# A two-layer decoder trunk on one core: modulation slices summed by GpSimd and ScalarE, gates by VectorE, tokens scaled ahead of plain transposes

## The chip, the cores and the metric

The kernel runs on one core of a Trainium2 chip. The metric is device time in microseconds (us) of one execution. A difference below 0.3% (3.5 us) is treated as no difference. The engines are TensorE (PE in the rows, its weight loads PEld), VectorE (DVE), ScalarE (ACT), GpSimd (POOL) and SyncE (SP), whose queue issues nearly all loads.

## The reference, cut to what matters

One sequence of 256 tokens of width 1024 passes two layers. Each layer has a token mixer and a channel mixer, the second being a dense SwiGLU in layer 0 and eight experts of which each token takes two in layer 1. Ahead of each mixer the tokens are normed and modulated by a vector `c`:

```python
c_act = jax.nn.silu(c)
for layer in range(DEPTH):
    mod = c_act @ ada_w[layer] + ada_b[layer]
    sh_m, sc_m, gt_m, sh_f, sc_f, gt_f = [m[:, None, :] for m in jnp.split(mod, 6, axis=-1)]
    h = modulate(rms_norm(x, norm_mix_g[layer]), sh_m, sc_m)
    x = x + gt_m * hybrid_mixer(h, ...)
    h = modulate(rms_norm(x, norm_ffn_g[layer]), sh_f, sc_f)
    x = x + gt_f * (swiglu(h, ...) if layer % 2 == 0 else moe_swiglu(h, ...))
return rms_norm(x, final_g)
```

`c_act @ ada_w` is twelve products of a vector of 1024 with a matrix of 1024 x 1024: twelve slices, named by kind (`sh_m`, `sc_m`, `gt_m`, `sh_f`, `sc_f`, `gt_f`) and layer. A shift or scale is wanted as a column (features along partitions), a gate as a row spread over all partitions. All inputs are float32.

## The kernel before

**Tiling.** Every weight comes in units of 128 x 2048 numbers (1 MB), loaded by SP into a ring of six buffers `raw` in the order in which the program loads them. Apart from the modulation's, a unit is split in two halves of 1024 columns: ScalarE rounds a half into `whi` (L145), VectorE subtracts into `wlo` (L146), and TensorE takes three products (high by high, high by low, low by high) for each block of weights. Five `whi` and five `wlo` buffers stand between the splits and TensorE.

**Stages.** The front is startup, mixer 0 (ten units of `win`, gated linear attention and a recurrence, four units of `wout` in `residual`), the dense layer (eleven pairs of units `f1` and `f3`, then eleven units `f2` in `residual`), and mixer 1. The experts follow. Each `residual` ends with four blocks of twelve products; after each block VectorE multiplies by the gate (`y`, L440) and adds into the tokens `xs` (L441). For two token halves `norm` then squares and sums on ScalarE (`junk`, L338), adds on VectorE (`rs`, L344), takes the power on GpSimd (L345), and multiplies the identity by the result on VectorE (`dg`, L360). TensorE multiplies the tokens by `dg` (L364), which turns and scales them at once; ScalarE applies scale and shift (`h`, L377), VectorE splits into `wide_hi` and `wide_lo` (L380, L381), and the next mixer starts.

**Modulation.** A slice is four loads of 1 MB, its pieces. They are queued by `put`, and `fill(n)` takes n pieces at places given by the table FILLS. The table ON says who works a slice. Seven of the twelve are products on TensorE with `c` repeated in 32 columns (L261): each piece is four products, laid side by side in four column groups. Five are multiplied and added on VectorE, two instructions for a piece (L264, L266), and then summed over partitions by products with ones (L276, L286). A column slice ends in four small transposes (L226 into `pm`, from `row`), a gate in two products that spread it (L276 or L278).

**Order.** The program is written in one order; a scheduler moves instructions on each engine before the kernel is built, and each engine then runs its own list strictly in order. A GpSimd instruction or a ScalarE instruction whose input is late thus holds all that stand behind it.

## Time and profile before

| | us |
|---|---|
| median of 3 runs (1166.84 to 1169.84) | 1167.07 |
| the profiled execution | 1168.7 |
| its span, first to last instruction | 1166.9 |
| startup, until mixer 0's first `win` product | 44.07 |
| mixer 0, until its last product | 104.74 |
| wait and norm between mixer 0 and the dense layer | 9.66 |
| dense layer, until its last product | 197.08 |
| wait and norm between dense layer and mixer 1 | 14.20 |
| mixer 1 | 97.55 |
| experts and last norm | 699.60 |

The stages are cut at TensorE's instructions, and their times add up to the span. The profiled execution is 1.6 us above the median, and 1.8 us of its time lie outside its span. TensorE's share of busy time is 95% over the span; it is a busy share of records that overlap, so a saving is read from the stage in which it falls.

### The profile page before, as it was taken

What the parts mean: (1) busy time and instruction counts of PE and PEld (TensorE: products, weight loads), DVE (VectorE), ACT (ScalarE), POOL (GpSimd) and SP (SyncE); (2) the same over time, 40 slices, a digit from 0 to 9 for tenths busy, and PEclk for the clock granted to TensorE, in tenths of its full rate; (3) what the DMA queues carried; (4) which work ended last, traced back from release to release, by engine and by line L of the source; (5) the groups of instructions that cost most, each with busy time, mean ns of one, the idle gap of its engine ahead of it and who ended that gap; (6) DMA issues with size and microseconds to landing.
All of it is one profiled execution on the core that took longest, in us unless ns stands there. A gap on an engine that the chain in (4) does not pass through costs nothing.

```text
span 1166.9 us, 15801 instructions
## 1 busy us (share of the span) xinstructions
PE 1107.4 (95%) x6125; PEld 742.8 (64%) x6125; DVE 627.4 (54%) x818; ACT 518.3 (44%) x724; POOL 30.5 (3%) x69
## 2 busy tenths in 40 slices
PE   4899999999999999899999999999999999998993
PEld 2578779999777888686465445554455544655540
DVE  2668556757776765797135443353343633345442
ACT  2764444444437744786234333542342333434331
POOL 2000000000001000300000000000000000000000
PEclk9899999999999999899999999999999999998996
DMA  9977486858886447495999999999999999999994
GB/s 361 410 288 291 145 324 249 310 201 306 334 332 229 147 143 288 181 359 189 418 420 419 420 419 420 419 420 420 388 406 419 420 419 419 419 419 403 398 420 172
DMA packets 57182, 395.69 MB, mean 339 GB/s; under 512 B 8294, under 2 KB 8710, under 8 KB 9356
## 3 DMA queue, kind: packets, MB, share of 16 engines
q1 hardware_dynamic: 54272, 393.24, 84.2%
q10 hardware_dynamic: 2828, 1.37, 0.4%
q8 instruction: 50, 0.82, 0.3%
q14 instruction: 32, 0.26, 0.1%
HBM read 393.53 MB, written 1.05 MB: 338 GB/s over the span
## 4 chain that ended last, share of the span: by engine, by line
PE 88%; DMA 4%; ACT 3%; DVE 2%; POOL 1%; issue 1%; ACTq 0%; POOLq 0%; DVEq 0%; SPq 0%
PE pa L1050 17%; PE pa L158 8%; PE pa L157 8%; PE pa L159 8%; PE po L1099 7%; PE pa L406 6%; PE pa L407 6%; PE pa L408 6%; PE pb L158 4%; PE pb L159 4%; PE pb L157 4%; PE pm L226 2%; PE pb L261 2%; PE pm L973 2%; DMA bdx<-in_wx_dram 2%; ACT whi L145 2%
## 5 line engine op out<-in xcount | busy, mean ns | idle before, releaser
L146 DVE TENSOR_TENSOR wlo<-raw,whi 128x1024 fp32r<-128x1024 f32 x318 | 378.6, 1222 | 205.1 <-ACT whi L145 204.4
L145 ACT ACTIVATE whi<-raw 128x1024 fp32r<-128x1024 f32 x318 | 324.5, 1057 | 214.7 <-PE pa L407 90.2
L1050 PE MATMUL pa<-raw,x_n 128*64 128x512 f32 (+3 forms) x960 | 205.0, 562 | 0.0
L406 PE MATMUL pa<-wide_hi,whi 128*128 128x256 f32 x544 | 154.3, 284 | 0.2 <-DVE wide_hi L380 0.2
L407 PE MATMUL pa<-wide_lo,whi 128*128 128x256 f32 x544 | 153.5, 282 | 0.2 <-DVE wide_lo L381 0.2
L408 PE MATMUL pa<-wide_hi,wlo 128*128 128x256 f32 x544 | 153.5, 282 | 0.0
L1050 PEld LDWEIGHTS pa<-raw,x_n 128*64 128x64 f32 (+1 forms) x960 | 63.0, 131 | 106.7 <-issue 101.3
L158 PE MATMUL pa<-wlo,x_hi 128*128 128x512 f32 (+1 forms) x288 | 113.3, 394 | 3.7 <-DVE wlo L146 3.7
L157 PE MATMUL pa<-whi,x_hi 128*128 128x512 f32 (+1 forms) x288 | 110.7, 389 | 0.9 <-ACT whi L145 0.3
L159 PE MATMUL pa<-whi,x_lo 128*128 128x512 f32 (+1 forms) x288 | 109.9, 382 | 0.1
L406 PEld LDWEIGHTS pa<-wide_hi,whi 128*128 128x128 f32 x544 | 102.3, 188 | 6.4 <-issue 4.0
L407 PEld LDWEIGHTS pa<-wide_lo,whi 128*128 128x128 f32 x544 | 102.5, 189 | 1.6 <-issue 1.1
L408 PEld LDWEIGHTS pa<-wide_hi,wlo 128*128 128x128 f32 x544 | 102.5, 188 | 0.3 <-issue 0.3
L1099 PE MATMUL po<-raw,big 128*64 128x512 f32 (+1 forms) x440 | 93.4, 616 | 6.3 <-DMA raw<-in_m_dram 6.3
L1053 ACT ACTIVATE s<-pa 128x512 f32<-128x512 f32 (+1 forms) x30 | 16.9, 562 | 163.4 <-PE pa L1050 163.4
L158 PE MATMUL pb<-wlo,a_hi 128*128 128x512 f32 x176 | 71.6, 408 | 2.0 <-DVE wlo L146 2.0
L158 PEld LDWEIGHTS pa<-wlo,x_hi 128*128 128x128 f32 x288 | 55.3, 192 | 26.5 <-DVE wlo L146 6.7
L159 PE MATMUL pb<-whi,a_lo 128*128 128x512 f32 x176 | 69.8, 398 | 0.0
L157 PEld LDWEIGHTS pa<-whi,x_hi 128*128 128x128 f32 x288 | 55.3, 192 | 21.8 <-issue 7.7
L157 PE MATMUL pb<-whi,a_hi 128*128 128x512 f32 x176 | 60.8, 403 | 2.0 <-ACT whi L145 2.0
L1099 PEld LDWEIGHTS po<-raw,big 128*64 128x64 f32 (+1 forms) x440 | 25.4, 132 | 57.8 <-issue 49.8
L159 PEld LDWEIGHTS pa<-whi,x_lo 128*128 128x128 f32 x288 | 55.5, 193 | 10.0 <-DVE x_lo L986 0.8
(323 smaller groups left out, 1242.4 us busy)
## 6 DMA issues: line engine op xcount, KB each, us to landing
raw<-in_m_dram SPq DMA_DIRECT2D x263, 1024.0 KB, 10.6
raw<-in_ada_w_dram SPq DMA_DIRECT2D x48, 1024.0 KB, 7.3
raw<-in_f_dram SPq DMA_DIRECT2D x33, 1024.0 KB, 6.0
raw<-in_win_dram SPq DMA_DIRECT2D x20, 1024.0 KB, 6.3
raw<-in_wout_dram SPq DMA_DIRECT2D x8, 1024.0 KB, 6.1
xs<-in_x_dram SPq DMA_DIRECT2D x1, 1024.0 KB
big<-in_m_dram SPq DMA_DIRECT2D x1, 1024.0 KB
out_dram<-big SPq DMA_DIRECT2D x2, 512.0 KB, 3.2
```

Of the source, the lines that this page charges most:

```text
L145: act.activation(hi[:, :n], src, AF.Copy)
L146: dve.tensor_tensor(lo[:, :n], src, hi[:, :n].bitcast(F32), op=ALU.subtract)
L157: pe.matmul(ps, l_hi, r_hi, start=first, stop=False)
L158: pe.matmul(ps, l_hi, r_lo, start=False, stop=False)
L159: return pe.matmul(ps, l_lo, r_hi, start=False, stop=last)
L226: return pe.transpose(o, i, ident[:i.shape[0], :i.shape[0]])
L261: pe.matmul(ps[o:o + 32, :], cact[:, k, :], wi[:, h * 512:(h + 1) * 512], start=(j == 0), stop=(j == 3))
L406: pe.matmul(pv[:, b, :], wh, h_hi[:, k, :], start=(k == 0), stop=False)
L407: pe.matmul(pv[:, b, :], wh, h_lo[:, k, :], start=False, stop=False)
L408: pe.matmul(pv[:, b, :], wl, h_hi[:, k, :], start=False, stop=(k == KD - 1))
L1050: pe.matmul(ps[r:r + m, :n], x_n[:, k, :], w[:, kk * n:(kk + 1) * n], start=(k < js), stop=(k >= KD - js))
L1099: pe.matmul(acc[r:r + m, :], aa["a_n"][:, k, :], w[:, i * 1024 + c * 512:i * 1024 + (c + 1) * 512], start=(k < js), stop=(k >= KF - js))
```

## The change

Six of the twelve slices (`sh_f` and `sc_f` of layer 0; `sh_m`, `sc_m`, `sh_f`, `sc_f` of layer 1) are laid out transposed in memory, so that a row holds all inputs of one output. GpSimd multiplies each half of a piece by `crow`, the vector `c_act` spread over all partitions, and ScalarE copies the product onto itself while it sums each row: the sum is the wanted column, without TensorE. The sums of a piece are taken at the next piece's place and behind the latest split; the multiplications stand behind the latest power. All four gates are worked on VectorE. Two slices at startup stay on TensorE. In `norm` the tokens of a half are first multiplied by their norm, 512 columns on VectorE and 512 on ScalarE (`tn`), and then turned by plain transposes; the factor 32 goes into the gains once, on GpSimd. `residual` now takes all pieces that are left and fetches the next norm ahead of its last blocks. At the start the first splits wait for the last modulation column. The places of the pieces change.

```diff
-LATE_ADA = 0
-AT_DENSE = 4
-ON = ((False,), (False,), (True,), (True,), (True,), (True,), (False,), (False,), (False,), (True,))
-FILLS = ((2, 1, 1, 1, 1, 1, 1, 1, 1, 2), (0, 0, 1, 3, 0, 0, 0, 0, 0, 0))
+AT_DENSE = 2
+SUMMED = ((0, "sh_f"), (0, "sc_f"), (1, "sh_m"), (1, "sc_m"), (1, "sh_f"), (1, "sc_f"))
+FILLS = ((0, 1, 1, 1, 1, 1, 1, 1, 1, 0), (0, 0, 0, 0, 1, 1, 1, 1, 0, 0))
+FILLS_D = ((0, 1, 0, 0, 1, 0, 0, 1, 0, 0, 0), (1,) * 11)
...
+    crow = const([P, D], F32, "crow", pre)
+    for h in range(2):
+        cp = pm()
+        for k in range(4):
+            pe.matmul(cp[:, k * P:(k + 1) * P], cs[:, 4 * h + k:4 * h + k + 1].to_broadcast([P, P]), ident[:],
+                      start=True, stop=True)
+        act.activation(crow[:, h * 512:(h + 1) * 512], cp[:], AF.Copy)
...
+    def ada_summed(layer, kind):
+        n = KINDS.index(kind)
+        m = mod_col(layer, kind)
+        todo = []
+        def sum_up():
+            with ExitStack() as order:
+                for i in last_split:
+                    order.enter_context(tc.issue_after(i.ins))
+                for w, b in todo:
+                    act.activation(w, w, AF.Copy, accum_out=m[:, b:b + 1])
+            todo.clear()
+        for j in range(4):
+            w = load(ada_w[layer, n, j])
+            halves = [(w[:, i * D:(i + 1) * D], 2 * j + i) for i in range(2)]
+            with ExitStack() as order:
+                for i in last_pow:
+                    order.enter_context(tc.issue_after(i.ins))
+                for wi, _ in halves:
+                    pool.tensor_tensor(wi, wi, crow[:], op=ALU.mult)
+            sum_up()
+            todo.extend(halves)
+            yield
...
-            dg = pre.tile([P, P], F32, tag=f"dg{t}", name=nm("dg"))
-            dve.tensor_scalar(dg[:], ident[:], rs[:], 32.0, op0=ALU.mult, op1=ALU.mult)
...
-            for k in range(KD):
-                pe.matmul(turned[k // 2][:, (k % 2) * SEQ + t * P:(k % 2) * SEQ + (t + 1) * P],
-                          xs[:, t, k * P:(k + 1) * P], dg[:], start=True, stop=True)
+            for j in range(2):
+                tn = pre.tile([P, 4, P], F32, tag="tn", name=nm("tn"), bufs=2)
+                half = xs[:, t, j * 512:(j + 1) * 512].rearrange("p (k s) -> p k s", k=4)
+                if j == 0:
+                    dve.tensor_scalar(tn[:], half, rs[:], None, op0=ALU.mult)
+                else:
+                    act.activation(tn[:], half, AF.Copy, scale=rs[:])
+                for i in range(4):
+                    k = 4 * j + i
+                    transpose(turned[k // 2][:, (k % 2) * SEQ + t * P:(k % 2) * SEQ + (t + 1) * P], tn[:, i, :])
...
-            hold((n0,), *((n, *m) for n, m in zip(ns, marks)))
+            hold((n0, *modded) if alone else (n0,), *((n, *m) for n, m in zip(ns, marks)))
...
         parts = parts_of(len(units) - 2) + parts_of(len(units) - 1)
+        rest()
+        block = next_block()
...
-    put(ada(0, "gt_m", *ON[0]), ada(0, "sh_f", *ON[1]), ada(0, "sc_f", *ON[2]))
+    put(ada(0, "sh_f"), ada(0, "sc_f"), ada(0, "gt_m"))
...
-    put(ada(1, "sh_m", *ON[8]), ada(1, "sc_m", *ON[8]), ada(0, "gt_f", *ON[3]), ada(1, "gt_m", *ON[4]), ada(1, "sh_f", *ON[5]),
-        ada(1, "sc_f", *ON[9]))
+    put(ada(1, "sh_m"), ada(1, "sc_m"), ada(1, "sh_f"), ada(0, "gt_f"), ada(1, "gt_m"), ada(1, "sc_f"))
...
+        for layer, kind in SUMMED:
+            i = KINDS.index(kind)
+            t = w[layer, i].T.reshape(4, 2, P, D).transpose(0, 2, 1, 3)
+            u[layer, i] = t.reshape(4, P, 2 * D)
```

**The order, in three places.** A row is line, operation, output, inputs and size of the output; a number behind x counts equal rows that follow each other, and a number behind a name is the buffer's.

TensorE between mixer 0's last product (first row) and the dense layer's first, before (L261 is the modulation, L364 the tokens by `dg`):

```order
L159 MATMUL pa_1131<-whi_1216,ee_1095 128x512
L261 MATMUL pb_1343<-raw_1344,cact 32x512 x4
L261 MATMUL pb_1343<-raw_1350,cact 32x512 x4
L261 MATMUL pb_1343<-raw_1356,cact 32x512
L364 MATMUL pm_1260<-dg_1258,xs 128x128 x2
L364 MATMUL pm_1261<-dg_1258,xs 128x128 x2
L364 MATMUL pa_1262<-dg_1258,xs 128x128 x2
L364 MATMUL pa_1263<-dg_1258,xs 128x128 x2
L261 MATMUL pb_1343<-raw_1356,cact 32x512 x3
L261 MATMUL pb_1343<-raw_1362,cact 32x512 x4
L261 MATMUL pb_1448<-raw_1449,cact 32x512 x4
L364 MATMUL pm_1260<-dg_1310,xs 128x128 x2
```

The same place after the change:

```order
L162 MATMUL pa_1094<-whi_1198,ee_1073 128x512
L229 MATMUL pa_1250<-ident,tn_1258 128x128 x2
L229 MATMUL pa_1251<-ident,tn_1258 128x128 x2
L229 MATMUL pm_1248<-ident,tn_1252 128x128 x2
L229 MATMUL pm_1249<-ident,tn_1252 128x128 x2
L229 MATMUL pm_1248<-ident,tn_1302 128x128 x2
L229 MATMUL pm_1249<-ident,tn_1302 128x128 x2
L229 MATMUL pa_1250<-ident,tn_1308 128x128 x2
L229 MATMUL pa_1251<-ident,tn_1308 128x128 x2
L443 MATMUL pa_1352<-wide_hi_1208,whi_1356 128x256
```

The five modulation pieces are gone, and nothing stands in their place.

VectorE in the norm between dense layer and mixer 1, from the third block's `y` to the last half's factor, before:

```order
L440 TENSOR_TENSOR y_3265<-pa_2817,gate_f 128x512
L344 TENSOR_SCALAR rs_3236<-ss_3216 128x1
L441 TENSOR_TENSOR xs<-xs,y_3265 128x512
L360 TENSOR_SCALAR dg_3239<-ident,rs_3236 128x128
L146 TENSOR_TENSOR wlo_3418<-raw_3411,whi_3417 128x1024
L440 TENSOR_TENSOR y_3283<-pa_2818,gate_f 128x512
L441 TENSOR_TENSOR xs<-xs,y_3283 128x512
L344 TENSOR_SCALAR rs_3288<-ss_3268 128x1
L360 TENSOR_SCALAR dg_3291<-ident,rs_3288 128x128
```

The same place after (L478 is `y`, L479 the sum into `xs`, L299 a gate's multiplication, L397 `tn`):

```order
L478 TENSOR_TENSOR y_3248<-pa_2794,gate_f 128x512
L376 TENSOR_SCALAR rs_3217<-ss_3197 128x1
L299 SCALAR_TENSOR_TENSOR acc_3719<-raw_3722,cs,acc_3719 128x1024
L479 TENSOR_TENSOR xs<-xs,y_3248 128x512
L397 TENSOR_SCALAR tn_3224<-xs,rs_3217 128x512
L149 TENSOR_TENSOR wlo_3390<-raw_3383,whi_3389 128x1024
L299 SCALAR_TENSOR_TENSOR acc_3719<-raw_3722,cs,acc_3719 128x1024
L478 TENSOR_TENSOR y_3266<-pa_2795,gate_f 128x512
L479 TENSOR_TENSOR xs<-xs,y_3266 128x512
L376 TENSOR_SCALAR rs_3271<-ss_3251 128x1
L397 TENSOR_SCALAR tn_3274<-xs,rs_3271 128x512
```

Two multiplications of the last gate now stand ahead of the last `y`. Two more stand further down, between the first casts into `wide_hi`.

ScalarE in the dense layer's pairs, before (L145 splits, L699 and L704 close a pair):

```order
L704 ACTIVATE a_hi<-s_1574 128x512
L145 ACTIVATE whi_1780<-raw_1774 128x1024
L145 ACTIVATE whi_1842<-raw_1834 128x1024
L699 ACTIVATE s_1703<-pa_1643 128x512
L145 ACTIVATE whi_1846<-raw_1834 128x1024
```

After (L271 is the sum of a multiplied half):

```order
L740 ACTIVATE a_hi<-s_1547 128x512
L148 ACTIVATE whi_1755<-raw_1749 128x1024
L271 ACTIVATE raw_1682,sc_m_1554<-raw_1682 128x1024 x2
L148 ACTIVATE whi_1817<-raw_1809 128x1024
L735 ACTIVATE s_1678<-pa_1618 128x512
L148 ACTIVATE whi_1821<-raw_1809 128x1024
L271 ACTIVATE raw_1811,sc_m_1554<-raw_1811 128x1024 x2
```

The sums stand between splits, and read what GpSimd has multiplied.

## Rows read from the trace of the kernel before

**Rows 1.** The page: what the DMA engines moved, in 40 slices of 29.2 us.

```profile
GB/s 361 410 288 291 145 324 249 310 201 306 334 332 229 147 143 288 181 359 189 418 420 419 420 419 420 419 420 420 388 406 419 420 419 419 419 419 403 398 420 172
```

**Rows 2.** Stages: stretch, length, PE, PEld, DVE, ACT, POOL, clock, DMA share, GB/s.

```profile
0.00:44.07 44.07, 24.63 (x148) 11.71 (x148) 15.89 (x54) 15.38 (x29) 5.90 (x23) 0.88 0.98 380
44.07:148.81 104.74, 104.74 (x661) 83.74 (x661) 73.83 (x102) 61.62 (x83) 3.15 (x3) 1.00 0.67 256
148.81:158.47 9.66, 9.43 (x73) 5.03 (x72) 4.65 (x9) 3.83 (x10) 0.55 (x1) 1.00 0.85 333
158.47:355.55 197.08, 196.85 (x1368) 178.35 (x1368) 135.58 (x139) 87.91 (x104) 1.82 (x2) 1.00 0.77 288
355.55:369.75 14.20, 13.43 (x102) 7.79 (x101) 10.78 (x20) 8.60 (x17) 3.68 (x7) 1.00 0.92 324
```

**Rows 3.** The chain of waits in order of time: start us, us, what.

```profile
42.59 0.38 ACT fl L475
...
50.03 1.00 PE pb L261 x8
...
92.25 0.99 PE pb L261 x8
...
130.41 0.87 PE pm L226 x8
...
137.10 0.98 PE pm L286 x4
...
153.56 2.71 PE pb L261 x22
...
165.16 0.99 PE pb L261 x8
...
174.31 0.44 PE pm L226 x4
...
201.92 0.99 PE pb L261 x8
...
326.68 0.39 PE pm L226 x4
...
356.21 0.61 DVE y L440
```

**Rows 4.** Groups by line, shapes apart: count, busy us, mean ns, idle before.

```profile
L146 DVE TENSOR_TENSOR wlo<-raw,whi 128x1024 fp32r<-128x1024 f32 x318 | 378.6, 1222 | 205.1 <-ACT whi L145 204.4 <-PE pb L261 0.2
L145 ACT ACTIVATE whi<-raw 128x1024 fp32r<-128x1024 f32 x318 | 324.5, 1057 | 214.7 <-PE pa L407 90.2 <-PE pa L159 74.4 <-DMA raw<-in_m_dram 38.5
...
L266 DVE SCALAR_TENSOR_TENSOR acc<-raw,cs,acc 128x1024 f32<-128x1024 f32 x37 | 47.4, 1281 | 11.1 <-DMA raw<-in_ada_w_dram 7.6 <-DMA acc<-in_ada_b_dram 3.1
...
L338 ACT ACTIVATION_READ_ACCUMULATOR junk<-xs 128x1 f32 x20 | 3.7, 186 | 0.0
```

**Rows 5.** Timeline behind mixer 1, VectorE and GpSimd: start, us, instruction.

```profile
476.53 3.45 POOL L869 TENSOR_SCALAR key<-cnt 128x8 f32<-128x8 f32 x1 [5.74 <-ACT cnt L867]
...
477.51 2.36 DVE L146 TENSOR_TENSOR wlo<-raw,whi 128x1024 fp32r<-128x1024 f32 x2
...
480.06 0.21 POOL L870 TENSOR_TENSOR key<-key,idx 128x8 f32<-128x8 f32 x1
...
480.50 0.29 POOL L880 TENSOR_TENSOR pm<-key 128x64 f32<-128x64 f32 x1
...
483.36 0.33 POOL L884 TENSOR_TENSOR pe<-pm,idx 128x64 f32<-128x64 f32 x1
```

**Rows 6.** Busy time in the dense pairs, columns as in rows 2.

```profile
160.00:180.00 20.00, 20.00 (x169) 19.02 (x168) 11.68 (x16) 10.08 (x14) 0.00 (x0) 1.00 0.87 336
```

**Rows 7.** VectorE's timeline in the norm ahead of the dense layer.

```profile
153.40 0.29 DVE L360 TENSOR_SCALAR dg<-ident,rs 128x128 f32<-128x128 f32 x1 [0.66 <-POOL rs L345]
157.99 0.43 DVE L380 CAST wide_hi<-h 128x512 fp32r<-128x512 f32 x1 [4.31 <-ACT h L377]
```

**Rows 8.** Busy time in a stretch with little work for TensorE.

```profile
476.00:480.00 4.00, 3.73 (x17) 3.68 (x17) 4.00 (x7) 1.42 (x5) 3.45 (x1) 0.50 1.02 426
```

More of the change, by code (lines that the diff above doesn't have):

```diff
@@ new lines, in trunk, with mod_col, finished @@
+    for o, n in ((_COLS["nmg"][0], 16), (_COLS["nfg"][0], 8)):
+        pool.tensor_scalar(cv[:, o:o + n], cv[:, o:o + n], 32.0, None, op0=ALU.mult)
+    def mod_col(layer, kind):
+        return cst.tile([P, KD], F32, tag=f"{kind}{layer}", name=f"{kind}{layer}")
+    def finished(layer, kind, m, last):
+        if kind[:2] == "sc":
+            last = dve.scalar_tensor_tensor(m[:], m[:], 1.0, col("nmg" if kind == "sc_m" else "nfg", 8 * layer, 8),
+                                            op0=ALU.add, op1=ALU.mult)
+        mod[kind, layer] = m
+        modded[:] = [last]
@@ new lines, in ada_summed @@
+    def ada_summed(layer, kind):
[20 more added lines that the diff above has]
+            yield
+        sum_up()
+        last = dve.tensor_tensor(m[:], m[:], col("ab", 48 * layer + 8 * n, KD), op=ALU.add)
+        finished(layer, kind, m, last)
+        yield
@@ L253, in ada, with ada_gate @@
+    def ada_gate(layer, kind):
+        n = KINDS.index(kind)
+        acc = pre.tile([P, D], F32, tag="acc", name=nm("acc"))
+        pool.memset(acc[:], 0.0)
+        act.dma_start(acc[0:1, :], ada_b[layer:layer + 1, n * D:(n + 1) * D])
         for j in range(4):
@@ new lines, in ada_gate, with ada_products @@
+                dve.scalar_tensor_tensor(acc[:], w[:, i * D:(i + 1) * D], cs[:, 2 * j + i:2 * j + i + 1], acc[:],
+                                         op0=ALU.mult, op1=ALU.add)
+            yield
+        dst = gate_m if kind == "gt_m" else gate_f
+        for h in range(2):
+            bp = pm()
+            pe.matmul(bp[:], ones[:], acc[:, h * 512:(h + 1) * 512], start=True, stop=True)
+            act.activation(dst[:, h * 512:(h + 1) * 512], bp[:], AF.Copy)
+        yield
+    def ada_products(layer, kind):
+        n = KINDS.index(kind)
+        ps = pb()
+        for j in range(4):
+            w = load(ada_w[layer, n, j])
+            for i in range(2):
+                for h in range(2):
+                    o = 64 * i + 32 * h
+                    pe.matmul(ps[o:o + 32, :], cact[:, 2 * j + i, :], w[:, i * D + h * 512:i * D + (h + 1) * 512],
+                              start=(j == 0), stop=(j == 3))
+            yield
+        row = wk.tile([P, 512], F32, tag="s", name=nm("row"))
+        act.activation(row[:], ps[:], AF.Copy)
+        tp = pm()
+        for b in range(4):
+            transpose(tp[:, b * P:(b + 1) * P], row[:, b * P:(b + 1) * P])
+        tv = tp[:].rearrange("p (b i h c) -> p c i h b", i=2, h=2, c=32)[:, 0]
+        m = mod_col(layer, kind)
+        mv = m[:].rearrange("p (h b) -> p h b", h=2)
+        bv = col("ab", 48 * layer + 8 * n, KD).rearrange("p (h b) -> p h b", h=2)
+        dve.tensor_tensor(mv, tv[:, 0], bv, op=ALU.add)
+        finished(layer, kind, m, dve.tensor_tensor(mv, tv[:, 1], mv, op=ALU.add))
@@ L304, in ada @@
         yield
+    def ada(layer, kind):
+        how = ada_gate if kind[:2] == "gt" else ada_summed if (layer, kind) in SUMMED else ada_products
+        return how(layer, kind)
     queue = []
@@ L424, in parts_of @@
             w = load(units[u])
-            if left() > keep:
-                fill(n_fill)
+            fill(n_fill)
             return [split(w[:, i * 1024:(i + 1) * 1024]) for i in range(2)]
@@ L685, in mixer, with dense @@
                                          op0=ALU.mult, op1=ALU.subtract)
-            rest()
-            residual([wout[layer, i] for i in range(4)], m_hi, m_lo, gate_m, next_block())
-    def dense(layer, per_unit, h_hi, h_lo, next_block):
+            residual([wout[layer, i] for i in range(4)], m_hi, m_lo, gate_m, next_block, n_fill=1)
+    def dense(layer, fills, h_hi, h_lo, next_block):
         fill(AT_DENSE)
@@ L705, in dense @@
                 dve.tensor_tensor(a_lo[:, o, :], sv, a_hi[:, o, :].bitcast(F32), op=ALU.subtract)
-            last = residual([f2[i] for i in range(11)], a_hi, a_lo, gate_f, next_block(), n_fill=1, keep=LATE_ADA)
-            with tc.issue_after(last.ins):
-                rest()
+            residual([f2[i] for i in range(11)], a_hi, a_lo, gate_f, next_block, n_fill=1)
     ready = {}
@@ L1298, in trunk @@
     hs = {}
-    put(ada(0, "sh_m", *ON[7]), ada(0, "sc_m", *ON[7]))
+    put(ada(0, "sh_m"), ada(0, "sc_m"))
     fill(X_AT)
```

93 lines of the change are left out of this document (19 added, 74 removed).

## The prediction

> **What bounds the kernel now.** I read the page's row of moved data first. From slice 19, some 554 us into the span, the DMA engines move 417 to 420 GB/s in most slices until the last [rows 1]: the experts wait for their weights, and those are loaded in one fixed order. The front moves 145 to 360 GB/s in most of its slices. So what the front loses or gains shifts the experts' loads, and the end, nearly one for one; I take it so and give the experts no term.
>
> Next I cut the front into stages [rows 2]. In mixer 0 TensorE is busy for 104.74 of 104.74 us, in the dense layer for 196.85 of 197.08, while VectorE works 73.83 and 135.58 us there, and ScalarE 61.62 and 87.91. The clock is granted in full (1.00). In these two stages only TensorE's work counts: an instruction that leaves it is worth its own time, as long as the engine that takes it over stays below the stage. The two norms are another matter: TensorE is busy in 9.43 of 9.66 us and in 13.43 of 14.20, but much of that is modulation that fills a wait. The chain of waits says what sets the end: it runs over the modulation's pieces in the stages, and in the second norm over VectorE's `y` at 356.21 [rows 3].
>
> **The change, part by part.** The sum is made against the profiled execution, 1168.7 us, of which 1166.9 are span; the median of the runs is 1167.07, 1.6 below it.
>
> *Mixer 0.* The chain shows six pieces of modulation inside the stage, the first 1.00 us at 50.03, the last 0.99 at 92.25, 5.84 us in all. Eight transposes of the row slices (0.87) and the four products that sum a slice over partitions (0.98) go too [rows 3]. The two gates' spreads cost the same before and after. 5.84 + 0.87 + 0.98 = 7.7 us less.
>
> *Dense layer.* Three pieces at 0.99 to 1.00, the first at 165.16, the last at 201.92; three groups of four transposes, 0.44 us at 174.31, 0.44, and 0.39 at 326.68; and one 0.98 for a sum as above [rows 3]: 2.98 + 1.27 + 0.98 = 5.2 us less.
>
> *Who takes the work over.* ScalarE sums 48 halves. One is an activation of 128x1024 (1057 ns) with the read of an accumulator (186 ns) [rows 4]: 1.24 us. 16 of them fall in mixer 0: 61.62 + 16 x 1.24 = 81 of 97 us that remain. 32 fall in the dense layer: 87.91 + 39.7 = 128 of 192. VectorE multiplies 32 halves at 1281 ns for the gates, against 40 multiplications before [rows 4], mostly fewer in the dense layer. Neither engine becomes the bound by its sum.
>
> GpSimd's 48 multiplications of 128x1024 have no row. Nearest are its products of two tensors: 0.21 us for 128x8, 0.29 to 0.33 for 128x64 [rows 5]. The growth is 0.08 to 0.12 us for 56 columns, 1.43 to 2.14 ns for one, so 0.21 + 1016 x 1.43 = 1.66 us up to 0.21 + 1016 x 2.14 = 2.39 us. I take 2.2, towards the longer row, which is the nearer one. In mixer 0 16 of these are 27 to 38 us, in the first eight dense pairs 24 are 40 to 57. A pair of 96 products lasts 96 / 169 x 20 = 11.36 us [rows 6], so eight last 91, some 85 of them before the last of these sums is due. GpSimd alone is hidden at either end.
>
> The Trainium skill, "GPSIMD Engine Reference", section "Elementwise — side-by-side cycle accounting", gives 4497 ns for an addition of 2048 columns; half, an estimate from that page, is 2.25 us for one multiplication. No run before the change shows that size. By it the 24 would take 54 us, and the sum stays as it is.
>
> But the two engines may not work side by side. Behind mixer 1 a GpSimd instruction on 128x8 (with a scalar) lasts 3.45 us, from 476.53 to 479.98; VectorE's two `wlo` run from 477.51 to 479.87, and GpSimd's next instruction, as small, takes 0.21 [rows 5]. If GpSimd and VectorE take turns, the eight pairs hold 24 x 1.66 to 2.39 of the one and 32 `wlo` at 1.222 = 39.1 of the other [rows 4]: 79 to 96 us in 85. At my 2.2 it is 92. The five split buffers hold a pair's work and a quarter, about 14 us, and cover that; so I put down only +1.5 us, for splits that come late here and there (bounds 0 and 15, below).
>
> The Trainium skill, "SBUF — State Buffer", section "Terms", calls the port pair of these two engines a lock held for a full instruction, the loser blocking fully. The row at 476.53 agrees in kind. By that rule without buffers the sum would be 7 us slower, and rival C is what it leads to.
>
> *Startup.* ScalarE's copy `fl` at 42.59 (0.38 us) stands on the chain ahead of mixer 0's first product [rows 3]. After the change the first splits wait for the last modulation column, which stops them from standing ahead of it; but a sum (1.24) and later splits stand ahead of `fl`. Two more activations at 1.06 and one sum at 1.24 are 3.4 us; `wlo` no longer stands ahead of the last modulation column, which I put at two of 1.22 us, 2.5: +0.9 us, bounds -2 and +2.
>
> *Norm ahead of the dense layer.* Before, five pieces fill it, half of them (2.71 us at 153.56) between the two halves' transposes, and they delay the second half [rows 3]. Without them the first `h` could follow VectorE's `dg` at 153.40 [rows 7] at once, 2.5 us earlier. Against this VectorE's list now puts one more `wlo` (1.22) ahead of the last factor, and `tn` of 512 columns, which I price by the cast of as many (0.43 us [rows 7]), takes the place of `dg` (0.29), with the wider wait for it: +1.9 (1.22 + 0.43 + 0.2 for the longer copy on ScalarE). Together -0.7 us, bounds -2.5 and +1.5.
>
> *Norm ahead of mixer 1.* The chain runs over `y` at 356.21 [rows 3], and two gate multiplications of 1.28 us now stand ahead of it (see the order above): +2.6, less 0.3 that VectorE waited there. Two more stand between the casts, for which TensorE waits next: +2.6. Of the four pieces and the sum over partitions that leave TensorE in this norm most fill waits; I take 0.7 as on the path. +4.2 us, bounds 0 and +6.
>
> *The clock.* Without pieces TensorE idles some 5 us in each norm. Where it has had little to do, the granted clock falls: 0.50 from 476 to 480 us [rows 8], and it is 0.88 over the startup [rows 2], while both norms have 1.00. At half the clock, 3 us of products take 1.5 more; I take half of this in each norm: +1.5 us, bounds 0 and 4.
>
> *Mixer 1* has none of the modulation's pieces on TensorE now, and the gate's last four multiplications in it (5.1 us of VectorE's time) have the room that VectorE has in mixer 0 [rows 2]: 0.
>
> The sum: +0.9 - 7.7 - 0.7 - 5.2 + 4.2 + 0 + 1.5 + 1.5 = -5.5. 1168.7 - 5.5 = 1163.2 on the profiled execution's basis, 1161.5 as a median.
>
> **The rivals.** *B, all is gained.* GpSimd and VectorE run side by side, the gate's multiplications in the second norm fall into its waits, and the clock holds: -7.7 - 5.2 = -12.9, so 1154. For it speaks that VectorE is idle for a third of the dense layer [rows 2]; against it, that the order puts two multiplications straight ahead of `y`.
>
> *C, the turn-taking decides, slower.* In the eight pairs the splits come late: at 2.39 us GpSimd and VectorE together need 96 us of 85, 11.4 too many. A `wlo` that is late holds TensorE, and ScalarE, which stands in order at a sum, does not even cut the next `whi`. In mixer 0, 16 x 2.39 + 73.83 = 112 of 97 us, of which buffers and waits absorb most: some +4. 1161.5 - 1.5 + 11.4 + 4 = 1175. It decides from about 2.0 us for a multiplication upwards (24 x 2.0 + 39.1 = 87), and only if the engines take strict turns and the buffers don't cover it. The row at 476.53 speaks for turns; the length of a multiplication is open.
>
> *D, the freed time becomes other waits.* ScalarE runs strictly in order, and a sum whose product GpSimd has not yet finished holds the next split. If this costs about half a sum's time at every second piece (12 x 0.6 = 7 us over the front), the saving is gone: 1167. That `whi` waits mostly for TensorE and not for its data before the change (214.7 us idle, 90.2 and 74.4 of it for TensorE [rows 4]) speaks against it, as there is time to spare.
>
> **How the numbers follow.** A difference of 0.3%, 3.5 us, is what a measurement of this kernel tells from none. The forecast, 1161.5, has 0.45, with a range of its own of 1158 to 1164.5, from the bounds of startup and the norms; B has 0.22, D 0.13, C 0.20. Faster: B wholly, and of the forecast all but what reaches above 1163.6, 0.38: 0.60. Same: that rest of the forecast (0.07) and D (0.13): 0.20. Slower: C, 0.20. The range takes in B at 1154 with 2 us below it, and C at 1175 with 1 above it: 1152 to 1176; what is left out is a startup or norm far off, and a C without any cover.
>
> **What would show it.** Right: mixer 0 near 97 us and the dense layer near 192, both with TensorE busy throughout; the multiplication at 1.7 to 2.4 us; the second norm near 18. Wrong: TensorE idle in the pairs for `wlo` or `whi`, a `wlo` well over 1.22 us while GpSimd multiplies, or multiplications longer than 3 us. Then C or D holds, by whether `whi` waits for a sum or `wlo` for GpSimd. A shorter second norm speaks for B. If the stages all shrink and the end does not, the experts' loads do not follow the front, and rows 1 were misread.

## The result and the profile after

The changed kernel takes 1223.47 us (median of 4 runs, 1221.07 to 1228.56) beside 1167.57 for the kernel before (now four runs): the ratio is 1.048, interval 1.044 to 1.052, so it is 56 us slower. The forecast was 1161.5, the range ended at 1176, and the rival with the right sign, C, stood at 1175.

The stages of the profiled execution (1221.43 us, of which 1219.7 are span), cut at the start of each stage's first and the end of its last product. Columns as in [rows 2]; the two last rows are mixer 1 and the experts. Cut in the same way, the stages of the kernel before are 44.07, 104.81, 9.60, 197.14, 14.06, 97.81 and 699.41 us, up to 0.3 us from the table of the profile before; from here on these are the ones compared.

```profile
0.00:52.79 52.79, 25.77 (x132) 11.73 (x132) 24.73 (x53) 20.59 (x38) 16.72 (x29) 0.77 0.82 317
52.79:173.73 120.94, 102.23 (x601) 85.36 (x600) 93.62 (x98) 72.45 (x106) 35.56 (x14) 0.92 0.59 222
173.73:187.06 13.33, 3.93 (x16) 3.13 (x17) 9.48 (x12) 6.94 (x14) 8.92 (x5) 0.68 0.46 159
187.06:400.75 213.69, 202.19 (x1328) 184.50 (x1328) 173.60 (x123) 116.35 (x163) 92.36 (x33) 0.94 0.71 271
400.75:420.35 19.60, 8.76 (x44) 5.87 (x44) 14.36 (x21) 9.93 (x19) 2.83 (x6) 0.65 0.52 179
420.35:523.22 102.87, 100.97 (x623) 87.00 (x623) 65.44 (x91) 58.83 (x80) 3.81 (x12) 0.97 0.52 195
523.22:1219.70 696.48, 657.21 (x3158) 370.53 (x3155) 325.02 (x410) 282.13 (x406) 11.65 (x21) 0.98 0.94 386
```

Each stage of the front is longer, and TensorE waits in each: it is busy for 102.23 us in 120.94 of mixer 0 and for 202.19 in 213.69 of the dense layer. The front takes 55.7 us more. The experts nearly keep their length (2.9 us less), as read from [rows 1], so the loss is all in the front. VectorE is busy for 93.62 us in mixer 0 and 173.60 in the dense layer, 20 and 38 more than in [rows 2], with fewer instructions. Its instructions have become longer. In the groups by line (columns as in [rows 4]):

```profile
L149 DVE TENSOR_TENSOR wlo<-raw,whi 128x1024 fp32r<-128x1024 f32 x318 | 411.3, 1328 | 183.2 <-ACT whi L148 182.1 <-DMA raw<-in_m_dram 0.2
...
L281 POOL TENSOR_TENSOR raw<-raw,crow 128x1024 f32<-128x1024 f32 x48 | 137.6, 2895 | 80.6 <-DMA raw<-in_ada_w_dram 63.8 <-DVE lf L523 7.1 <-DVE a_lo L741 6.3
...
L418 DVE TENSOR_TENSOR wide_lo<-h,wide_hi 128x512 fp32r<-128x512 f32 x12 | 20.5, 1719 | 0.3
```

A GpSimd multiplication takes 2.9 us in the mean with its waits, and `wide_lo`, 0.69 us when nothing disturbs it, takes 1.72. The 48 multiplications last between 2.34 and 3.42 us each (shortest, median and longest in ns):

```profile
L281 POOL TENSOR_TENSOR raw<-raw,crow x48: 2343/2824/3415, 37.6 to 369.2; 128x1024 f32<-128x1024 f32 x48
```

The timeline of startup says why, VectorE and then GpSimd:

```profile
37.23 0.42 DVE L417 CAST wide_hi<-h 128x512 fp32r<-128x512 f32 x1
37.69 2.84 DVE L418 TENSOR_TENSOR wide_lo<-h,wide_hi 128x512 fp32r<-128x512 f32 x1
40.45 2.58 DVE L417 CAST wide_hi<-h 128x512 fp32r<-128x512 f32 x1
43.07 2.73 DVE L418 TENSOR_TENSOR wide_lo<-h,wide_hi 128x512 fp32r<-128x512 f32 x1
45.72 2.58 DVE L417 CAST wide_hi<-h 128x512 fp32r<-128x512 f32 x1
48.33 0.69 DVE L418 TENSOR_TENSOR wide_lo<-h,wide_hi 128x512 fp32r<-128x512 f32 x1
...
37.63 10.38 POOL L281 TENSOR_TENSOR raw<-raw,crow 128x1024 f32<-128x1024 f32 x4 [23.08 <-DMA raw<-in_ada_w_dram]
```

Four multiplications last 10.38 us, 2.6 each with the turns that VectorE takes between them, and VectorE ends four instructions, one behind each; when the fourth multiplication is over, at 48.01, the next one is short again. Each of VectorE's instructions waits until a whole multiplication has ended, and GpSimd's next multiplication waits for it in turn. These casts are on the chain of waits, and mixer 0 starts 8.7 us late (5.2 of it by the multiplications, see e2). The same in mixer 0's recurrence and in the norm ahead of the dense layer, VectorE and GpSimd:

```profile
81.28 1.21 DVE L149 TENSOR_TENSOR wlo<-raw,whi 128x1024 fp32r<-128x1024 f32 x1
82.41 0.68 DVE L564 TENSOR_TENSOR ee<-ee,pa 128x512 f32<-128x512 f32 x1
83.01 0.67 DVE L565 TENSOR_TENSOR ee<-ee,pa 128x512 f32<-128x512 f32 x1
83.61 3.86 DVE L559 SCALAR_TENSOR_TENSOR ur<-xp,cv,ur 128x256 f32<-128x256 f32 x2
...
81.44 5.75 POOL L281 TENSOR_TENSOR raw<-raw,crow 128x1024 f32<-128x1024 f32 x2 [0.56 <-DMA raw<-in_ada_w_dram]
...
181.88 25.95 POOL L281 TENSOR_TENSOR raw<-raw,crow 128x1024 f32<-128x1024 f32 x10
```

Two instructions that read one input from PSUM (`ee` with `pa`) keep their 0.68 us beside a running multiplication; the next with both inputs in SBUF waits. In the norm and on into the dense layer ten multiplications stand behind each other, from 181.88 to 207.83, and behind the first cast the casts and subtractions there take 2.58 to 2.75 us each. A stretch of the recurrence and the first 20 us of the dense layer show what this does to TensorE:

```profile
72.79:97.79 25.00, 10.11 (x64) 8.79 (x63) 25.00 (x25) 13.68 (x22) 16.56 (x6) 0.70 0.70 266
187.06:207.06 20.00, 11.80 (x48) 10.21 (x49) 18.44 (x7) 7.38 (x15) 20.00 (x8) 0.59 0.28 105
```

In the recurrence VectorE is busy all the time, much of it waiting, and TensorE for 10.11 of 25.00 us; in both stretches the granted clock falls (0.70 and 0.59).

### The profile page after: what moved, and what is told of

The parts are those of the page before. It is cut to its first block, busy times and chain, and to the rows that moved or that the text cites. A ratio compares the mean times of both kernels' runs of the same rounds, so it can differ in the third digit from the quotient of the medians.

```text
span 1219.7 us, 15532 instructions
## 1 busy us (share of the span) xinstructions
PE 1101.1 (90%) x5897; PEld 748.1 (61%) x5897; DVE 706.3 (58%) x803; ACT 567.2 (47%) x822; POOL 171.8 (14%) x119
## 4 chain that ended last, share of the span: by engine, by line
PE 75%; DVE 12%; DMA 5%; ACT 3%; issue 3%; POOL 1%; POOLq 0%; ACTq 0%; DVEq 0%
PE pa L1084 16%; PE pa L161 7%; PE pa L160 7%; PE pa L162 7%; PE po L1133 7%; PE pa L443 4%; PE pa L444 4%; PE pa L445 4%; PE pb L161 4%; PE pb L162 4%; PE pb L160 4%; DVE wlo L149 3%; PE pm L229 2%; DMA fl<-in_winf_dram 2%; PE pm L1007 1%
## 5 line engine op out<-in xcount | busy, mean ns | idle before, releaser
L149 DVE TENSOR_TENSOR wlo<-raw,whi 128x1024 fp32r<-128x1024 f32 x318 | 411.3, 1328 | 183.2 <-ACT whi L148 182.1
L444 PE MATMUL pa<-wide_lo,whi 128*128 128x256 f32 x544 | 156.6, 288 | 6.5 <-DVE wide_lo L418 6.5
L443 PE MATMUL pa<-wide_hi,whi 128*128 128x256 f32 x544 | 157.2, 290 | 2.2 <-DVE wide_hi L417 2.2
L281 POOL TENSOR_TENSOR raw<-raw,crow 128x1024 f32<-128x1024 f32 x48 | 137.6, 2895 | 80.6 <-DMA raw<-in_ada_w_dram 63.8
L377 POOL TENSOR_TENSOR rs<-rs,mhalf 128x1 f32<-128x1 f32 x10 | 10.4, 1037 | 747.0 <-DVE rs L376 744.0
L444 PEld LDWEIGHTS pa<-wide_lo,whi 128*128 128x128 f32 x544 | 105.3, 194 | 7.7 <-DVE wide_lo L418 7.6
L443 PEld LDWEIGHTS pa<-wide_hi,whi 128*128 128x128 f32 x544 | 104.8, 193 | 4.5 <-DVE wide_hi L417 3.1
L445 PEld LDWEIGHTS pa<-wide_hi,wlo 128*128 128x128 f32 x544 | 105.9, 195 | 1.0 <-DVE wlo L149 1.0
```

Source lines behind the costliest of these rows:

```text
L149: dve.tensor_tensor(lo[:, :n], src, hi[:, :n].bitcast(F32), op=ALU.subtract)
L281: pool.tensor_tensor(wi, wi, crow[:], op=ALU.mult)
L443: pe.matmul(pv[:, b, :], wh, h_hi[:, k, :], start=(k == 0), stop=False)
L444: pe.matmul(pv[:, b, :], wh, h_lo[:, k, :], start=False, stop=False)
L445: pe.matmul(pv[:, b, :], wl, h_hi[:, k, :], start=False, stop=(k == KD - 1))
```

## The experiments

Three theories were set against each other after the result. Theory 1: a GpSimd multiplication shuts VectorE out. Theory 2: the sums on ScalarE and the load buffers held longer starve the splits and loads. Theory 3: the new norm, the gates or the places of the pieces cost the time. What each run's stages lost or gained against the kernel before, in us, worked out from the stage rows of both profiles (spans; the last column is the run's ratio to the kernel before with its interval):

| | startup | mixer 0 | norm 1 | dense | norm 2 | mixer 1 | experts | ratio |
|---|---|---|---|---|---|---|---|---|
| changed kernel | +8.7 | +16.1 | +3.7 | +16.6 | +5.5 | +5.1 | -2.9 | 1.048 (1.044 to 1.052) |
| e1 products | +0.3 | +1.2 | -0.9 | +12.0 | +12.0 | +6.9 | +1.1 | 1.026 (1.024 to 1.029) |
| e2 short | +3.5 | -5.7 | +2.8 | -2.7 | +5.8 | +6.3 | | |
| e3 VectorE | +3.8 | +9.9 | +4.1 | -2.4 | +6.2 | +6.0 | -2.3 | 1.021 (1.019 to 1.023) |
| e4 norm | -0.9 | +1.5 | -1.2 | 0.0 | +0.4 | -1.3 | 0.0 | 1.000 (0.999 to 1.001) |
| e5 pairs | +1.2 | +1.2 | +1.6 | +7.9 | +11.1 | +6.7 | -3.6 | 1.022 (1.021 to 1.024) |
| e6 held | +0.6 | +26.1 | +1.3 | +14.3 | +5.6 | +4.2 | -1.2 | 1.042 (1.040 to 1.044) |
| e7 two slices | +0.9 | +0.1 | -0.2 | -4.4 | +5.6 | -1.3 | 0.0 | 1.001 (1.000 to 1.002) |
| e8 gate | -0.4 | 0.0 | 0.0 | 0.0 | +2.8 | +8.8 | -1.6 | 1.008 (1.006 to 1.011) |
| e9 fill | +9.7 | +1.7 | +3.6 | -2.2 | +6.0 | +6.9 | | |
| e10 later | -0.2 | +1.6 | -0.2 | -4.4 | +5.9 | -1.2 | +0.6 | 0.999 (0.998 to 1.001) |
| e11 one slice | 0.0 | 0.0 | -0.9 | -4.0 | +1.7 | 0.0 | +0.4 | 0.998 (0.997 to 0.999) |
| e12 sums | +8.5 | +9.0 | +1.6 | +18.4 | +6.4 | +5.7 | | |

In e2, e9 and e12 part of the modulation is left out, so the experts get other tokens; only their front is compared (their totals are 1344.63, 1604.42 and 1623.06 us; e9 and e12 ran once). A stage of a single execution is known to some 1.5 us: e7 and e10, whose programs are the same up to the dense layer, differ by as much in mixer 0.

**e1, the slices back on TensorE.**

```diff
-SUMMED = ((0, "sh_f"), (0, "sc_f"), (1, "sh_m"), (1, "sc_m"), (1, "sh_f"), (1, "sc_f"))
+SUMMED = ()
```

> All six slices go back to products on TensorE, at the places, with the gates and the norm of the changed kernel; GpSimd multiplies nothing and ScalarE sums nothing. Theory 1 (each GpSimd multiplication shuts VectorE out for its 2.6 us, which is lost where VectorE stands on the chain: first casts, recurrence, norms): 1165 to 1175 us. Theory 2 (the sums on ScalarE, and pieces that hold their load buffers longer, starve the loads): as low, so this run does not part it from theory 1. Theory 3 (the norm with plain transposes, the gates on VectorE or the places of the pieces): stays at 1200 or above.

1200.93 us. Startup, mixer 0 and the first norm are as before the change; the dense layer and what follows are not. It has 12.80 us of modulation pieces in the dense layer, where the kernel before had 3.20, and the second norm and mixer 1 lose 19 us without any GpSimd work. The time lies above the range of theories 1 and 2 and at the lower end of theory 3's. GpSimd's multiplications and ScalarE's sums together make 22.5 us of difference against these products, and 31 us of the front's loss are there without either. 9.6 of these are the pieces' own products in the dense layer; the 19 behind it are theory 3's, in part (e4 clears the norm, e8 measures the gate).

**e2, GpSimd's work cut short.**

```diff
-                    pool.tensor_tensor(wi, wi, crow[:], op=ALU.mult)
+                    pool.tensor_tensor(wi[:, :64], wi[:, :64], crow[:, :64], op=ALU.mult)
```

> The changed kernel, but GpSimd multiplies only the first 64 of each 1024 columns; the other columns are summed without being multiplied, so the modulation is left incomplete. Order, sums and buffers as in the changed kernel. Theory 1: nearly all of the loss goes with GpSimd's time: 1150 to 1165 us, a multiplication at about 0.3 us, first casts at 0.43 and 0.69 us. Theory 2: the sums and the held buffers stay, so 1205 or above.

With the order, buffers and sums of the changed kernel, the front ends at 477.4 us and not at 523.2. The length of the multiplications alone is worth 45.8 us. Its stage rows of mixer 0 and the dense layer:

```profile
47.61:146.70 99.09, 98.02 (x601) 83.74 (x600) 72.53 (x98) 73.01 (x108) 11.62 (x15) 0.98 0.68 259
...
159.09:353.52 194.43, 194.42 (x1328) 179.81 (x1328) 118.97 (x123) 112.79 (x156) 19.06 (x27) 0.99 0.77 293
```

Here the two savings of the prediction appear: -5.7 and -2.7 us, where 7.7 and 5.2 were worked out. VectorE's same 98 and 123 instructions take 72.53 and 118.97 us and not 93.62 and 173.60. The total was expected at 1150 to 1165 with the experts as they are; since they get other tokens it says nothing. What is left in the front is 10 us: 12.1 in the second norm and mixer 1 and 6.3 in startup and the first norm, less these two savings. Part of the 45.8 us is TensorE's clock: for the same 601 and 1328 products it is busy for 102.23 and 202.19 us in the changed kernel and for 98.02 and 194.42 here, where the granted clock is 0.98 and 0.99 and not 0.92 and 0.94. That is 12.0 us of slower products behind the waits.

**e3, the multiplications on VectorE.**

```diff
-                    pool.tensor_tensor(wi, wi, crow[:], op=ALU.mult)
+                    dve.tensor_tensor(wi, wi, crow[:], op=ALU.mult)
```

> The multiplications move from GpSimd to VectorE, in their places in the program; sums stay on ScalarE. Theory 1: a multiplication then costs VectorE 1.22 us in its own list and not 2.6 us of waiting, and the scheduler can place it behind what is urgent: 1165 to 1185 us. Theory 2: 1205 or above, as buffers are held as long.

1192.94 us, 30 less than on GpSimd, though VectorE now does all of it: 1.22 us in its own list costs less than being shut out for 2.34 or more. It is 8 us above the range that theory 1 gave and 12 below theory 2's; most of the loss is in mixer 0 (+9.9), where the multiplications stand in the recurrence.

**e4, the new norm alone.** In the kernel before, `dg` and its products give way to `tn`, plain transposes and gains times 32, as in the diff of the change.

> The kernel before with the new norm alone (tokens scaled ahead, plain transposes, gains times 32); modulation, gates and places as before. Theories 1 and 2: no cost in the norm itself, 1165 to 1170 us. Theory 3: 5 us or more slower than before.

1168.58 us beside 1168.75: no difference. The norm and the transposes are not the cause.

**e12, the sums cut short.**

```diff
-                    act.activation(w, w, AF.Copy, accum_out=m[:, b:b + 1])
+                    act.activation(w[:, :64], w[:, :64], AF.Copy, accum_out=m[:, b:b + 1])
```

> The changed kernel, but ScalarE sums only the first 64 of each 1024 columns; the rest is left out of the sums, so the experts get other tokens and only the time up to the end of mixer 1 is to be compared. GpSimd's work is whole. Theory 1 (VectorE shut out by GpSimd): the front stays near 520 us. Theory 2 (the sums hold ScalarE's splits): it falls to 490 or below.

The front ends at 517.2 us and not at 523.2. ScalarE's sums cost 6 us net, 7 of them in mixer 0: a tenth of the loss. The other half of theory 2, load buffers held longer, is tested by e9 below.

**e8, the last gate alone, in the kernel before.**

```diff
-ON = ((False,), (False,), (True,), (True,), (True,), (True,), (False,), (False,), (False,), (True,))
+ON = ((False,), (False,), (True,), (True,), (True,), (True,), (True,), (False,), (False,), (True,))
```

> The kernel before with one edit: the last gate (gt_f of layer 1), eight multiplications of 1.28 us, goes from TensorE to VectorE at its places. Theory 4 (this gate makes the norm ahead of mixer 1 and mixer 1's recurrence longer, which all changed versions show by 12 us): 1175 to 1180, the second norm near 20 us and mixer 1 near 104. Rival (it is hidden and those stages lose by something else): 1167 to 1170.

1177.94 us, 9.5 slower, and where theory 4 said: its rows of the second norm and mixer 1.

```profile
355.22:372.06 16.84, 12.08 (x70) 8.48 (x68) 10.29 (x18) 8.56 (x16) 3.78 (x7) 0.80 0.28 84
372.06:478.62 106.56, 103.50 (x623) 89.23 (x623) 70.26 (x97) 58.81 (x80) 3.80 (x12) 0.94 0.56 208
```

VectorE has 70.26 us of work in 106.56, and still the gate's multiplications, seven of them in this stage, lengthen it by 8.8: the chain of waits runs over VectorE's recurrence, and one of them stands on it. From mixer 1's chain in this run, and two stretches of it:

```profile
391.05 0.65 DVE ur L519 x2
391.70 0.08 DVE dec L506
391.78 1.19 DVE acc L266
392.97 0.79 DVE ur L522 x2
...
392.06:402.06 10.00, 6.94 (x45) 6.77 (x44) 10.00 (x15) 4.15 (x5) 0.00 (x0) 0.78 0.62 217
402.06:412.06 10.00, 10.00 (x35) 8.03 (x36) 4.53 (x9) 2.56 (x6) 0.00 (x0) 0.54 0.41 161
```

VectorE is busy throughout the first stretch while TensorE idles for 3.06 us, all that it idles in this stage; then its clock is granted at 0.54 for ten microseconds. The other 5.7 us of the 8.8 are the same 623 products at the lower clock (103.50 us busy, 97.81 before).

Moving this gate alone costs the two stages 11.5 us; the changed kernel loses 10.6 there. With e2 the 55.7 us by which the changed kernel's front is longer come apart: 45.8 of GpSimd's time, and, in e2's row, 12.1 in these two stages and 6.3 in startup and the first norm, less 8.4 saved in mixer 0 and the dense layer.

**e5, GpSimd in the dense pairs only.**

```diff
-AT_DENSE = 2
+AT_DENSE = 0
...
-SUMMED = ((0, "sh_f"), (0, "sc_f"), (1, "sh_m"), (1, "sc_m"), (1, "sh_f"), (1, "sc_f"))
+SUMMED = ((1, "sh_m"), (1, "sc_m"), (1, "sh_f"))
```

> The changed kernel with GpSimd's multiplications only in the dense layer's pairs (three slices of layer 1, the first piece at the first pair); the two slices of mixer 0 and the last one of layer 1 are products on TensorE. Theory 1 (a multiplication shuts VectorE out for its 2.6 us, and this costs only where VectorE stands on the chain): startup 44 to 45 us, mixer 0 about 106, dense layer below 200, as the five split buffers cover the waits there. The second norm and mixer 1 stay some 12 us longer than before, by the gate on VectorE; in all 1175 to 1185. Rival (the multiplications also cost in the pairs): dense layer 210 or more, 1195 or above.

1194.69 us. Startup and mixer 0 are normal again. The dense layer is 205.08, between the two theories' numbers; two stretches of it show where:

```profile
162.42:182.42 20.00, 16.05 (x94) 15.17 (x95) 13.42 (x8) 8.31 (x16) 10.21 (x4) 0.66 0.20 60
182.42:282.42 100.00, 99.91 (x833) 99.70 (x832) 91.81 (x63) 66.61 (x96) 56.38 (x18) 1.00 0.81 316
```

In the first 20 us the multiplications still meet the norm's casts: TensorE starves and its clock falls (0.66). In the 100 us of pairs behind it TensorE is busy for 99.91, with eighteen multiplications and VectorE at 92%. In the pairs turn-taking is covered when the multiplications are spread like this (e6 shows where that ends). The second norm is 11.1 us longer here, more than the gate costs in e8; see what is open below.

**e6, the multiplications held until the casts are done.**

```diff
+            held = wk.tile([P, 1], F32, tag="held", name=nm("held"))
+            last_pow[:] = [pool.tensor_tensor(held[:], h_lo[:, KD - 1, 0:1].bitcast(F32), mhalf[:, 0:1], op=ALU.mult)]
             n0, *ns = HOLD_N["f" if kind == "f" else layer]
```

> The changed kernel with one more GpSimd instruction behind each modulation, which reads the last of the split tokens, so that the next multiplications cannot start before the norm's casts are done; nothing is left out. Theory 1: startup falls from 52.8 to about 46 us, the first norm and dense layer together lose 15 us or more, mixer 0 stays near 120; in all 1195 to 1205. Theory 2 (held buffers starve the loads): as slow or slower, since the buffers are held longer.

1217.89 us, a miss by 13 us: startup falls to 44.69, but mixer 0 takes 130.93. The eight multiplications that waited run in a row from 41.87 to 65.21 and shut VectorE out where the recurrence begins. The first norm and the dense layer, which were to lose 15 us together, lose 4.7: there eighteen multiplications that waited run in a row from 191.29 to 247.90. Most of that stretch:

```profile
206.55:247.90 41.35, 31.97 (x254) 30.73 (x253) 38.64 (x17) 26.84 (x41) 41.35 (x13) 0.99 0.76 276
```

GpSimd multiplies without a pause, VectorE is busy for 93% of the time, and TensorE, in the pairs, idles for 9.4 us. Holding moves the loss. The pairs cover multiplications that are spread, not this row of them.

**e7 and e10, two slices in the pairs of the kernel before.** `sh_m` and `sc_m` of layer 1 are worked as in the change, with the instruction of e6, and AT_DENSE goes from 4 to 0. e10 also takes four pieces more in the last four pairs.

```diff
-    put(ada(1, "sh_m", *ON[8]), ada(1, "sc_m", *ON[8]), ada(0, "gt_f", *ON[3]), ada(1, "gt_m", *ON[4]), ada(1, "sh_f", *ON[5]),
+    put(ada_summed(1, "sh_m"), ada_summed(1, "sc_m"), ada(0, "gt_f", *ON[3]), ada(1, "gt_m", *ON[4]), ada(1, "sh_f", *ON[5]),
...
-                stationary_pair(p3[:], load_fill(f3[u], per_unit), h_hi, h_lo)
+                stationary_pair(p3[:], load_fill(f3[u], per_unit + (u >= 7)), h_hi, h_lo)
```

> The kernel before, but the two slices sh_m and sc_m of layer 1 are multiplied by GpSimd and summed by ScalarE in the dense layer's pairs, held until the casts of the norm are done; gates, norm and all else as before. Theory 1: three pieces and two groups of transposes leave TensorE in the dense layer, nothing else moves: 4 us less, 1162 to 1166. Rival (multiplications cost in the pairs too): 1170 to 1180.

> As the run before it with two slices in the pairs (e7), but four more pieces are taken in the last four pairs, so that fewer gate and scale multiplications are left for the end of the dense layer. If their lateness made that run's second norm 5 us longer: second norm back to 14 to 16 us, in all 1162 to 1166. Rival (the second norm is long for another reason, or the pairs have no more room): 1168 to 1172.

1169.49 and 1168.58 us, beside 1168.42 and 1169.04: nothing gained. The dense layer gives 4.4 us, where the prediction's prices for three pieces and two groups of transposes make 3.9, and the second norm takes them back. e10 was to show that late VectorE work does this; the norm stayed near 20 us. VectorE's rows from the kernel before (two), e7 and e10 show what is late in each, and the last row is a stretch of e10's norm:

```profile
349.16 0.69 DVE L440 TENSOR_TENSOR y<-pb,gate_f 128x512 f32<-128x512 f32 x1 [2.33 <-PE pb L159]
353.48 0.20 DVE L344 TENSOR_SCALAR rs<-ss 128x1 f32<-128x1 f32 x1
...
354.44 0.21 DVE L387 TENSOR_SCALAR rs<-ss 128x1 f32<-128x1 f32 x1
...
351.09 1.29 DVE L485 TENSOR_TENSOR y<-pb,gate_f 128x512 f32<-128x512 f32 x2 [2.90 <-PE pb L159]
...
355.00:360.00 5.00, 3.02 (x14) 3.05 (x15) 1.89 (x6) 1.45 (x4) 1.41 (x2) 0.58 1.00 333
```

In the kernel before, the first half's `rs` comes 2.1 us ahead of the dense layer's last product (355.62). In e7 it comes 2.5 us behind it (351.98): multiplications of a gate or scale, 1.27 us each, stand ahead of it in VectorE's list. In e10 these are out of the way, but the first `y` waits for TensorE until 1.4 us ahead of the last product (352.46), where the kernel before has it 6.5 us ahead: ScalarE waited 2.97 and 1.08 us for loads of the last dense units, and TensorE finished all four blocks nearly together. In the stretch shown VectorE has little to do, TensorE idles and its clock falls (0.58). The last gate's pieces fill this norm in all three (4.06 us before, 4.26 in e7, 5.06 in e10). That the loads are late because AT_DENSE takes no pieces ahead of the pairs was argued from the trace; e11 tests it.

**e11, one slice, all loads in step.** Only `sc_m` of layer 1 is moved; AT_DENSE stays 4.

```diff
-    put(ada(1, "sh_m", *ON[8]), ada(1, "sc_m", *ON[8]), ada(0, "gt_f", *ON[3]), ada(1, "gt_m", *ON[4]), ada(1, "sh_f", *ON[5]),
+    put(ada(1, "sh_m", *ON[8]), ada_summed(1, "sc_m"), ada(0, "gt_f", *ON[3]), ada(1, "gt_m", *ON[4]), ada(1, "sh_f", *ON[5]),
```

> The kernel before with one slice moved (sc_m of layer 1: GpSimd and ScalarE, one piece in each of the first four pairs, held until the casts are done); all other pieces keep their places, so the loads stay in step, four pieces still fill the norm ahead of the dense layer, and the last gate's pieces still fill the one ahead of mixer 1. If the freed time of the two runs with two slices (e7, e10) was lost because the gate's pieces came too late for that norm and TensorE stood idle there: dense layer 193 to 194 us, second norm 14 to 15, in all 3 us less than before, 1164 to 1167. Rival (any piece on GpSimd lengthens the second norm): second norm near 20, no gain.

1166.23 us beside 1168.68, ratio 0.998 (0.997 to 0.999): 2.4 us less, clear of the noise but below the 3.5 us that this document counts as a difference. The rows of the dense layer and the second norm:

```profile
157.62:350.75 193.13, 192.90 (x1344) 177.28 (x1348) 145.85 (x138) 94.06 (x119) 25.85 (x11) 1.00 0.78 295
350.75:366.52 15.77, 13.40 (x102) 7.63 (x101) 10.02 (x20) 8.46 (x16) 3.87 (x8) 1.00 0.90 311
```

The pieces fill the norm (13.40 of 15.77 us, clock 1.00), and most of the four microseconds of the dense layer are kept, as expected of the loads' lateness as cause. e11 differs from e7 in the number of slices as well as in AT_DENSE, so it fits that cause and does not single it out.

**e9, GpSimd fills instead of multiplying.**

```diff
-                    pool.tensor_tensor(wi, wi, crow[:], op=ALU.mult)
+                    for k in range(3):
+                        pool.memset(wi, 0.0)
```

> The changed kernel, but GpSimd fills each half with zeros three times (about 0.95 us each) where it multiplied it; the modulation is left out, so the experts get other tokens and only the time up to the end of mixer 1 is to be compared. As long on GpSimd as a multiplication, but it reads nothing. If VectorE is shut out by any GpSimd work of that length: casts at 2.5 us as in the changed kernel, startup 52 and mixer 0 near 120 us. If only GpSimd's reading shuts out VectorE's instructions with two inputs: wide_lo back near 0.7 us, mixer 0 near 100 and the front near 480.

Neither expectation holds as a whole. Startup stays at 53.7 us, while mixer 0 falls to 106.5, the dense layer to 194.9 and the front to 493.0, 30.2 us below the changed kernel's. VectorE and GpSimd at startup, then VectorE in the recurrence:

```profile
37.91 0.69 DVE L419 TENSOR_TENSOR wide_lo<-h,wide_hi 128x512 fp32r<-128x512 f32 x1
38.69 10.21 DVE L418 CAST wide_hi<-h 128x512 fp32r<-128x512 f32 x1
48.93 0.69 DVE L419 TENSOR_TENSOR wide_lo<-h,wide_hi 128x512 fp32r<-128x512 f32 x1
...
37.83 10.78 POOL L282 MEMSET raw<- 128x1024 f32 x12 [22.95 <-DMA raw<-in_ada_w_dram]
...
73.08 3.62 DVE L557 TENSOR_SCALAR ur<-xp,cv 128x256 f32<-128x256 f32 x2
```

A cast, with one input, waits until all twelve fills are over, 10.21 us; `wide_lo`, with two inputs, ran beside the first of them at its usual 0.69 (its 12 instances have a mean of 691 ns here, 1719 in the changed kernel), and `wlo` is back at 1230 ns up to 420 us (1569 there in the changed kernel). The sums wait for GpSimd and the load buffers are held about as long as in the changed kernel (three fills take 2.7 us), so neither of these makes the 30.2 us: they were waits of VectorE's instructions with two inputs in SBUF.

## Why the prediction was wrong

**What failed** is the step "The two engines may not work side by side": it saw the row at 476.53 [rows 5], found that the turns fit the dense pairs with the split buffers' cover, and put down +1.5 us, for the pairs; it was the only term for turns in the whole front. For mixer 0 the prediction said that neither VectorE nor ScalarE becomes the bound by its sum, and gave the turns nothing. The cover was checked in the pairs alone, and there it holds for spread multiplications (e5: 99.91 of 100 us; e7: -4.4 us; not for e6's row of eighteen). It was not checked at the places where VectorE itself is on the chain, which the same sum dealt with as if GpSimd were idle: startup's casts (+0.9 put down, +8.7 measured, 5.2 of it gone with the multiplications in e2), the recurrence of mixer 0 (-7.7 put down, +16.1 measured, -5.7 in e2), the casts of the first norm, which run into the dense layer (-5.2 put down, +16.6 measured, -2.7 in e2; of TensorE's 11.5 idle us there 8.2 lie in the first 20, and 3.3 between 344 and 373, where GpSimd's last slice meets a gate's multiplications). Together these are 46.3 us; the other stages give back 0.5, which leaves the 45.8 of e2.

**Rival C** had the right sign and the right mechanism, and too small a size at the wrong place. It charged the pairs with 11.4 us and mixer 0 with 4, as "buffers and waits absorb most". Buffers of splits can't absorb a late recurrence, since nothing in it was made ahead. Its sum for mixer 0 counted 16 multiplications, 112 us of VectorE and GpSimd in turns; 12 fall there (four ran in startup), and 12 x 2.34 with the 72.53 us that VectorE works there in e2 is 101, while the stage takes 120.94. So the sum over the stage does not give the loss either: the waits stand one behind the other on the chain.

**Rival D**, ScalarE held by a sum whose product is late, is not the cause: ScalarE idled for GpSimd's products four times, 7.0 us in all, and in e9, where the sums wait for GpSimd as long, mixer 0 and the dense layer get 33 us back.

**A multiplication** was taken as 2.2 us, with bounds of 1.66 and 2.39. The shortest of the 48 takes 2.34, so the term was 6% too small and inside its bounds; what is longer, up to 3.42, has one of VectorE's turns in it. The Trainium skill, "GPSIMD Engine Reference", section "Elementwise — side-by-side cycle accounting", from which 2.25 us were estimated, is within 4% of that shortest one. By neither figure would the forecast have changed sign.

**The gate in mixer 1** was a term of 0, argued from VectorE's free share. e8 measures +8.8 us in mixer 1 and +2.8 in the norm, for which +4.2 was put down. A share of a stage says nothing of an engine that carries the chain for a part of it.

**The clock** was put at +1.5 us, in the norms alone. It fell there (0.68 and 0.65), and in mixer 0 and the dense layer too (0.92 and 0.94), where slower products make 12.0 us. There is a slip in the term too: at half the clock 3 us of products take 3 us more, not 1.5.

**What held**: the experts shift with the front (696.5 us beside 699.4); the pieces' price on TensorE (e11: -4.0 us for what the prediction's prices give as 3.4); the two savings when GpSimd's time is gone (e2: -8.4 of -12.9); the plain transposes at about nothing (e4: 1.000); the second norm in its number (+5.5 beside +4.2), which is partly luck, as the gate alone makes +2.8 of it in e8.

**Open**: why the second norm is 12 us longer in e1 and 11 in e5 was read only from its chain (in e1 a wait of 9.2 us for a load of `win`, then two waits of 4.8 for pieces of the gate; in e5 nearly the same), and no run takes that apart. Nor does any run explain what e2 leaves in startup (+3.5, +0.9 put down) and in the first norm (+2.8, -0.7 put down): e12, with short sums, still has +8.5 in startup, and e4, the new norm alone, has -1.2 in the first norm.
